# The bias table moved between the forget chunks and the memory attention, two small products put into each of seven k-steps of the first chunk, and three additions of the last stage written for POOL

## The chip, the cores and the metric

One core of a Trainium2 chip runs the whole kernel. The number that counts is device time in microseconds (us) for one execution, from launch to end; it is measured several times on the chip, and the median stands for the kernel. One further execution is recorded by the hardware profiler, and every row below is from that one. Engines are named as the profile names them: PE (TensorE), DVE (VectorE), ACT (ScalarE), POOL (GpSimd), SP (SyncE, which only issues transfers here).

## The reference

A transformer block on 512 tokens of width 1024, all in float32. Three branches read the same x: a dilated band attention with a relative-position bias, a gated linear recurrence (HGRN), and an attention to a memory of 256 rows. Their gated sum is normalised, goes through a mixture of 32 experts (two per token), and is normalised again.

```python
proj = x @ w_in[l]
o_a  = dilated attention of pa with bias = rel_bias[bucket[i, j], head]
o_b  = hgrn2(pb): f = lb + (1 - lb) * sigmoid(f_raw); logf = log(f); bc = cumsum(logf)
o_c  = softmax(pc . k / sqrt(128)) . v        # k, v = mem @ w_kv, 4 heads
merged = gate0 * (o_a @ w_a) + gate1 * (o_b @ w_b) + gate2 * (o_c @ w_c)
x = layer_norm(DN_ALPHA * x + merged @ w_out)
x = layer_norm(DN_ALPHA * x + moe(x))         # two experts per token
```

## The kernel before

The layout is transposed: features lie on the 128 partitions, tokens on the free axis. Each product in full precision is made of three products of halves: a value `v` is split into `h` (rounded to fp32r on ACT, helper `split`, L83) and `l = v - h` (DVE, L84), and `product` adds h·h, h·l and l·h. So a weight chunk of 128 output columns (`proj`, L131) is a 512 KB load on SP's queue, one cast on ACT, one subtraction on DVE and 24 matmuls of 128x512 on PE. The tile pool `wp` gives the chunks rotating buffers (three for each half, four for the raw weights).

The program's order around the change:

- **Start.** Ten products of a zero tile (L151), then x is loaded in eight pieces `xr`; after each one its two halves are made and the three matmuls of that k-step of the first forget chunk go into `acc0` (L166).
- **Forget stage.** Seven more forget chunks. Each ends in a sigmoid (`forget`, L244) and later a logarithm (`log_sums`, L249) on ACT. The two functions need different tables, and ACT loads one before each (16 ACT_TABLE_LOAD in the stage). The memory's halves `mmh`, `mml` are made in between.
- **Memory attention.** For each of four heads: products q (24 of 128x512), k and v (24 of 128x256 each), then for four pieces of 128 rows scores `sc`, maximum, exponential (ACT L297), transposes and the product with v. Then two gate chunks.
- **Bias table.** In a pool of its own (`a0`, two buffers per tag): five pieces `bk` of a one-hot table come in by two POOL transfers each (L327), are cast on ACT (`bkr`, L329), multiplied with the bias table (PE L331, 12 output rows), copied from PSUM on ACT (`rows`, L333), and written to DRAM (`biasd`, POOL L334); later POOL spreads them from there (`repd`, L339).
- **HGRN.** Pool `b`, whose tiles (`bx`, `batt`, `bq`) lie on the same side of the memory as the tiles of `a0`.
- **Experts**, then the **last stage**: every token block c of 128 rows takes two rows picked back from DRAM, `back[c][0]` and `back[c][1]` (loads L1126). `both(c)` adds the two (L1181). `finish(c)` brings the sum to PSUM by a product with the identity (L1137) and adds the last experts (L1038); `norm_out(c)` is bn_stats (L1143), bn_aggr, a scaled subtraction (L1151) on DVE, and for c < 3 a multiplication on ACT (L1158) and an addition on POOL (L1159). In this stage the order on DVE and PE is the one written (`manual_schedule`); elsewhere the scheduler of the tile framework sets it. Every engine works its own list in order.

Of the kernel before, what the change touches and what calls it, by code (L numbers as in the profile page):

```python
# [10 lines left out]
F32 = mybir.dt.float32  # L11
# [9 lines left out]
NEG = -1.0e30  # L21
# [15 lines left out]
def build(tc, ins, out, dbg=None):  # L37
# [5 lines left out]
    def T(pool, shape, dt=F32, tag=None, **kw):  # L43
        cnt[0] += 1
        tag = tag or f"u{cnt[0]}"
        return pool.tile(list(shape), dt, name=f"{tag}_{cnt[0]}", tag=tag, **kw)
# [108 lines left out]
    with tc.tile_pool(name="xs", bufs=2, side="right") as xsp:  # L155
        for k in range(8):
            r = T(xsp, [128, 512], tag="xr", bufs=8)
            nc.sync.dma_start(r, ins["xT"][:, k, :])
            if k % 4 == 0:
                ws = slice(k * 128, (k + 4) * 128)  # L160
                nc.sync.dma_start(raw0[:, ws], ins["w_in"][36 + 8][:, ws])
                split(w0[0][:, ws], w0[1][:, ws], raw0[:, ws])
            split(xh[:, k, :], xl[:, k, :], r)
            ks = slice(k * 128, (k + 1) * 128)
            for n, (wt, m) in enumerate(((w0[0], xh), (w0[0], xl), (w0[1], xh))):
                TE.matmul(acc0, wt[:, ks], m[:, k, :], start=k == 0 and n == 0, stop=k == 7 and n == 2)  # L166

    lvlf = T(fp, [128, 6, 32], tag="lvl")
    G.dma_start(lvlf, ins["lvl"])
# [98 lines left out]
        log_sums(hd)  # L268


    och = T(op_, [128, 4, 512], F32R, tag="oh4")
    ocl = T(op_, [128, 4, 512], F32R, tag="ol4")
    with cpool:
# [32 lines left out]
    dump("oc", och.bitcast(F32))  # L306
    sgc = [gate(2, cb) for cb in range(2)]

    with tc.tile_pool(name="a0", bufs=2, side="right") as tp:
        tab = T(tp, [97, 12], tag="tab")
        V.memset(tab, 0.0)
        for r0 in (0, 64):
            V.memset(tab[r0:r0 + 33, :], NEG)
            G.dma_start(tab[r0:r0 + 32, :], ins["rel_bias"])
        tabr, tabh = (T(tp, [97, 12], F32R, tag=t) for t in ("tabr", "tabh"))
        S.copy(tabr[0:64, :], tab[0:64, :])
        S.copy(tabh, tab)
        V.tensor_tensor(tabr[64:97, :], tab[64:97, :], tabh[64:97, :].bitcast(F32), op=OP.subtract)  # L320
        for j in range(5):
            w = min(512, 2304 - j * 512)
            js = slice(j * 512, j * 512 + w)
            bk = T(tp, [97, 512], tag="bk")
            V.memset(bk[32:64, :w], 0.0)
            for r0 in (0, 64):
                G.dma_start(bk[r0:r0 + 33, :w], ins["bucket"][:, js])  # L327
            bkr = T(tp, [97, 512], F32R, tag="bkr")
            S.copy(bkr[:, :w], bk[:, :w])  # L329
            pt = bank("sc")  # L330
            TE.matmul(pt[:12, :w], tabr, bkr[:, :w], start=True, stop=True)  # L331
            rows = T(tp, [12, 512], tag="rows")
            S.copy(rows[:, :w], pt[:12, :w])  # L333
            G.dma_start(bias_d[:, js], rows[:, :w])  # L334

    def bias_copies(h):
        for lo, n, g, rows in ((0, 7, 0, 32), (7, 1, 1, 128), (8, 1, 2, 128)):
# [834 lines left out]
    with tc.manual_schedule(engines={mybir.EngineType.DVE, mybir.EngineType.PE}):  # L1172
        accs = [None] * 4

        def begin(c, n):
            if c < 3:
                add_to(accs[c][n], n, x1[:, c, :], True)
            add_up(accs[c][n], c, n, group[:1], c == 3, False)

        def both(c):  # L1180
            V.tensor_tensor(back[c][0], back[c][0], back[c][1], op=OP.add)  # L1181

        def finish(c):
            for n in range(2):
                add_to(accs[c][n], n, back[c][0] if c < 3 else x1[:, c, :], False)
            for n in range(2):
                add_up(accs[c][n], c, n, group[1:], False, True)

        def first(j):
            if j == 2:  # L1190
                accs[0] = [bank("sc"), bank("sc")]
                for n in range(2):
                    begin(0, n)
            else:
                accs[2], accs[1] = [bank("pj"), None], [bank("tr"), None]
                begin(2, 0)
                begin(1, 0)

        ohs = onehot(15)
        yp = T(mp, [128, 2, 1024], F32R, tag="yp")  # L1200
        group.append((ohs, yp))
        gu = gate_up(15, xs, first)
        sg = hidden(gu)
        hT = hidden_T(sg)
        both(0)
        accs[2][1] = bank("pj")
        begin(2, 1)
        dn = [down(15, n, hT) for n in range(2)]
        weighted(yp, dn[0], 15, 0)
        both(1)  # L1210
        weighted(yp, dn[1], 15, 1)
        accs[1][1] = bank("tr")
        begin(1, 1)
        finish(0)
        norm_out(accs[0], 0, False)
        both(2)
        finish(1)
        norm_out(accs[1], 1, False)
        both(3)
        V.tensor_tensor(x1[:, 3, :], x1[:, 3, :], back[3][0], op=OP.add)  # L1220
        finish(2)
        norm_out(accs[2], 2, False)
        accs[3] = [bank("o"), bank("o")]
        for n in range(2):
            begin(3, n)
        finish(3)
        norm_out(accs[3], 3, True)
# [98 lines left out]
```

## Time and profile before

| | us |
|---|---|
| median of three runs | 1138.49 |
| lowest, highest | 1136.7, 1140.42 |
| the profiled execution, its time | 1141.1 |
| its span, first to last instruction | 1138.7 |
| PE busy in it | 1087.6 (96%) |
| DVE, ACT, POOL busy | 492.2, 446.4, 82.6 |

The span is what the rows of the trace add up to; 2.4 us of the execution's time lie outside it. An engine's busy share alone decides nothing: it has to be read stage by stage, with what the engines wait for.

### The profile page before, as it was taken

What the parts mean: (1) busy time and instruction counts of PE and PEld (TensorE: products, weight loads), DVE (VectorE), ACT (ScalarE), POOL (GpSimd) and SP (SyncE); (2) the same over time, 40 slices, a digit from 0 to 9 for tenths busy, and PEclk for the clock granted to TensorE, in tenths of its full rate; (3) what the DMA queues carried; (4) which work ended last, traced back from release to release, by engine and by line L of the source; (5) the groups of instructions that cost most, each with busy time, mean ns of one, the idle gap of its engine ahead of it and who ended that gap; (6) DMA issues with size and microseconds to landing.
All of it is one profiled execution on the core that took longest, in us unless ns stands there. A gap on an engine that the chain in (4) does not pass through costs nothing.

```text
span 1138.7 us, 17136 instructions
## 1 busy us (share of the span) xinstructions
PE 1087.6 (96%) x6859; PEld 782.2 (69%) x6859; DVE 492.2 (43%) x985; ACT 446.4 (39%) x756; POOL 82.6 (7%) x107
## 2 busy tenths in 40 slices
PE   9999989999999999999999999999999999888884
PEld 6788778778888887887887887888776333332332
DVE  5554467777777323223223223336467111111126
ACT  7965556666666433233233233224114111111112
POOL 1000330000000000000000001000051211110003
PEclk9999999999999999999999999999999999999998
DMA  8742442222222432332331323633956999999992
GB/s 281 235 128 78 119 135 66 83 66 75 83 59 67 117 100 64 103 93 64 103 94 54 96 93 112 216 93 112 382 218 225 378 406 408 400 398 406 408 372 79
DMA packets 70482, 201.22 MB, mean 177 GB/s; under 512 B 16924, under 2 KB 19064, under 8 KB 70400
## 3 DMA queue, kind: packets, MB, share of 16 engines
q1 hardware_dynamic: 63216, 183.92, 46.1%
q0 software_dynamic: 7184, 16.17, 4.1%
q8 instruction: 55, 0.90, 0.3%
q14 instruction: 27, 0.22, 0.1%
HBM read 191.54 MB, written 17.81 MB: 184 GB/s over the span
## 4 chain that ended last, share of the span: by engine, by line
PE 80%; DMA 9%; ACT 6%; DVE 3%; issue 1%; POOL 0%; DVEq 0%; SPq 0%; ACTq 0%; POOLq 0%
PE pj L131 50%; PE pj L838 7%; DMA raw<-in_wexp_dram 7%; PE o L1054 4%; PE tr L222 3%; PE pj L765 2%; PE o L765 2%; ACT wh L83 1%; PE o L570 1%; PE sc L542 1%; PE sc L412 1%; ACT L244 1%; PE sc L548 1%; PE o L304 1%; ACT L249 1%
## 5 line engine op out<-in xcount | busy, mean ns | idle before, releaser
L84 DVE TENSOR_TENSOR wl<-raw,wh 128x1024 fp32r<-128x1024 f32 (+1 forms) x129 | 148.0, 1149 | 253.2 <-PE pj L131 188.3
L83 ACT CAST wh<-raw 128x1024 fp32r<-128x1024 f32 (+1 forms) x137 | 132.6, 969 | 234.5 <-PE pj L131 223.9
L131 PE MATMUL pj<-xh,wh 128*128 128x512 f32 x760 | 203.2, 401 | 3.7 <-ACT bw L352 3.5
L131 PE MATMUL pj<-xl,wh 128*128 128x512 f32 x760 | 196.6, 396 | 0.0
L131 PE MATMUL pj<-xh,wl 128*128 128x512 f32 x760 | 189.9, 392 | 0.0
L131 PEld LDWEIGHTS pj<-xh,wl 128*128 128x128 f32 x760 | 142.7, 188 | 31.1
L131 PEld LDWEIGHTS pj<-xh,wh 128*128 128x128 f32 x760 | 139.9, 189 | 33.4 <-ACT bw L352 3.9
L131 PEld LDWEIGHTS pj<-xl,wh 128*128 128x128 f32 x760 | 142.1, 189 | 29.6
L838 PE MATMUL pj<-raw,xs 128*64 128x512 f32 x432 | 118.5, 599 | 6.4 <-DMA raw<-in_wexp_dram 5.3
L838 PEld LDWEIGHTS pj<-raw,xs 128*64 128x64 f32 x432 | 35.1, 136 | 67.8 <-issue 46.0
L1054 PE MATMUL o<-raw,ehT 128*64 128x512 f32 x204 | 54.2, 617 | 1.2 <-ACT ehT L1064 0.5
L198 ACT ACTIVATE esg<-pj 128x256 f32<-128x256 f32 x16 | 6.2, 384 | 124.5 <-PE pj L838 124.5
L199 DVE SCALAR_TENSOR_TENSOR esg<-esg,pj 128x256 f32<-128x256 f32 x16 | 6.7, 420 | 107.3 <-ACT esg L198 107.3
L609 POOL DMA_DIRECT2D x<-in_xc_dram x4 | 2.1, 538 | 549.1 <-ACT oh L83 549.1
L1114 DVE TENSOR_SCALAR yp<-o,wsl 128x512 f32<-128x512 f32 x14 | 10.5, 750 | 65.5 <-PE o L1054 65.4
L1054 PEld LDWEIGHTS o<-raw,ehT 128*64 128x64 f32 x204 | 16.9, 140 | 28.2 <-issue 22.6
L131 PE MATMUL pj<-oh,wh 128*128 128x512 f32 x128 | 33.8, 393 | 1.4 <-issue 1.4
L131 PE MATMUL pj<-ol,wh 128*128 128x512 f32 x128 | 33.7, 393 | 0.0
L131 PE MATMUL pj<-oh,wl 128*128 128x512 f32 x128 | 33.3, 392 | 0.0
L214 DVE SCALAR_TENSOR_TENSOR sg<-sg,pj 128x512 f32<-128x512 f32 x16 | 11.0, 687 | 42.0 <-PE pj L131 42.0
L131 PEld LDWEIGHTS pj<-oh,wh 128*128 128x128 f32 x128 | 24.0, 188 | 6.5 <-issue 1.4
L131 PEld LDWEIGHTS pj<-oh,wl 128*128 128x128 f32 x128 | 24.0, 188 | 5.2
(399 smaller groups left out, 1460.8 us busy)
## 6 DMA issues: line engine op xcount, KB each, us to landing
raw<-in_wexp_dram SPq DMA_DIRECT2D x159, 512.0 KB, 10.8
raw<-in_w_in_dram SPq DMA_DIRECT2D x95, 512.0 KB, 3.6
wh<-in_wexp_dram SPq DMA_DIRECT2D x18, 512.0 KB, 11.0
wl<-in_wexp_dram SPq DMA_DIRECT2D x15, 512.0 KB, 12.2
yd<-merged SPq DMA_DIRECT2D x8, 512.0 KB, 7.0
raw<-in_w_kv_dram SPq DMA_DIRECT2D x8, 512.0 KB, 3.6
raw<-in_w_bb_dram SPq DMA_DIRECT2D x8, 512.0 KB, 3.6
raw<-in_w_out_dram SPq DMA_DIRECT2D x8, 512.0 KB, 3.7
```

The costliest lines, as they stand in the source:

```text
L83: S.copy(h, src)
L84: (eng or V).tensor_tensor(l, src, h.bitcast(F32), op=OP.subtract)
L131: TE.matmul(acc, wt[:, k * 128:(k + 1) * 128], m[:, k, :], start=n == 0, stop=n == 3 * kt - 1)
L222: TE.transpose(pt[:, j * 128:(j + 1) * 128], src[:, j * 128:(j + 1) * 128], ident)
L244: S.activation(nat(f), cls(acc), AF.Sigmoid)
L249: S.activation(f, f, AF.Ln, scale=oml[:, hd:hd + 1], bias=lb[:, hd:hd + 1])
L304: TE.matmul(o[:, cs], v[:, js], pT[:, js], start=j == 0, stop=j == 1)
L412: TE.matmul(sa4[g * 32:(g + 1) * 32, n, j], X[:, 2 + n, gs], X[:, 2 + n, gs], start=True, stop=True)
L542: TE.matmul(s1[g * 32:(g + 1) * 32, i * 256:(i + 1) * 256], qs[0][:, c * 128 + g * 32:c * 128 + (g + 1) * 32], ks[0][:, lows[g] * 128:lows ...
L765: TE.matmul(acc, m[:, k, cs], w[:, j * 512:(j + 1) * 512], start=k == 0 and n == 0, stop=k == 7 and n == 2)
L838: TE.matmul(acc[rows_, :], xs[:, j * 2 + k, rows_], raws[2 * p + q, j][:, k * 512:(k + 1) * 512], start=j == 0 and k == 0, stop=j == 3 and ...
L1054: TE.matmul(acc[rows_, :], hT[:, k * 128 + q * 64:k * 128 + (q + 1) * 64], raws[2 * p + q, 4 + k][:, n * 512:(n + 1) * 512], start=k == 0, ...
```

## The change

Three edits. In the start, after the three matmuls of each of the first seven k-steps, two 128x128 products of `xl` with itself go into the bank `tr`, whose contents nothing reads. The code of the bias table moves, unaltered in its arithmetic, from behind the memory attention to in front of it; its pool is gone: the small tables lie in the constant pool, `bk` and `rows` in three rotating buffers of the gate pool (tag `sg`), and `bkr` in `obl`. In the last stage `both(2)`, `both(3)` and the addition to `x1[:, 3, :]` are written ahead of `hidden` and for POOL.

```diff
             for n, (wt, m) in enumerate(((w0[0], xh), (w0[0], xl), (w0[1], xh))):
                 TE.matmul(acc0, wt[:, ks], m[:, k, :], start=k == 0 and n == 0, stop=k == 7 and n == 2)
+            if k < 7:
+                x0 = xl[:, k, 0:128].bitcast(F32)
+                for j in range(2):
+                    TE.matmul(pt, x0, x0, start=True, stop=True)
...
     for hd in range(NF):
         log_sums(hd)
+    tab = T(cp, [97, 12], tag="tab")
...
+    for j in range(5):
+        w = min(512, 2304 - j * 512)
+        js = slice(j * 512, j * 512 + w)
+        bk = T(gp, [128, 512], tag="sg")[:97]
+        V.memset(bk[32:64, :w], 0.0)
+        for r0 in (0, 64):
+            G.dma_start(bk[r0:r0 + 33, :w], ins["bucket"][:, js])
+        bkr = obl[:97, j, :]
+        S.copy(bkr[:, :w], bk[:, :w])
+        pt = bank("sc")
+        TE.matmul(pt[:12, :w], tabr, bkr[:, :w], start=True, stop=True)
+        rows = T(gp, [128, 512], tag="sg")[:12]
+        S.copy(rows[:, :w], pt[:12, :w])
+        G.dma_start(bias_d[:, js], rows[:, :w])
...
-    with tc.tile_pool(name="a0", bufs=2, side="right") as tp:
-        tab = T(tp, [97, 12], tag="tab")
...
-            G.dma_start(bias_d[:, js], rows[:, :w])
...
         def both(c):
-            V.tensor_tensor(back[c][0], back[c][0], back[c][1], op=OP.add)
+            (V if c < 2 else G).tensor_tensor(back[c][0], back[c][0], back[c][1], op=OP.add)
...
         gu = gate_up(15, xs, first)
+        both(2)
+        both(3)
+        G.tensor_tensor(x1[:, 3, :], x1[:, 3, :], back[3][0], op=OP.add)
         sg = hidden(gu)
...
         norm_out(accs[0], 0, False)
-        both(2)
         finish(1)
         norm_out(accs[1], 1, False)
-        both(3)
-        V.tensor_tensor(x1[:, 3, :], x1[:, 3, :], back[3][0], op=OP.add)
```

The order of instructions that results is known for both kernels; three places follow. In the rows, numbers behind names tell tiles apart, and x8 means eight alike in a row.

**Place 1, the end of the forget stage.** PE before, head 0 of the memory attention: k (mmh, mml with wh_547, wl_548), then v (wh_580, wl_581), then its scores.

```order
L131 MATMUL pj_544<-mmh_210,wh_547 128x256 x8
L131 MATMUL pj_544<-mml_211,wh_547 128x256 x8
L131 MATMUL pj_544<-mmh_210,wl_548 128x256 x8
L131 MATMUL pj_577<-mmh_210,wh_580 128x256 x8
L131 MATMUL pj_577<-mml_211,wh_580 128x256 x8
L131 MATMUL pj_577<-mmh_210,wl_581 128x256 x8
L291 MATMUL sc_615<-ck_543,cq_510 128x256
L291 MATMUL sc_632<-ck_543,cq_510 128x256
```

PE now: the same k, and inside its last eight products the bias piece 1 (L294); then v, and head 1's q (wh_763) where head 0's scores stood.

```order
L131 MATMUL pj_619<-mmh_224,wh_622 128x256 x8
L131 MATMUL pj_619<-mml_225,wh_622 128x256 x8
L131 MATMUL pj_619<-mmh_224,wl_623 128x256 x3
L294 MATMUL sc_548<-ol_13_100,tabr_528 12x512
L131 MATMUL pj_619<-mmh_224,wl_623 128x256 x5
L131 MATMUL pj_652<-mmh_224,wh_655 128x256 x8
L131 MATMUL pj_652<-mml_225,wh_655 128x256 x8
L131 MATMUL pj_652<-mmh_224,wl_656 128x256 x8
L131 MATMUL pj_767<-xh_81,wh_763 128x512 x3
```

The bias product of piece 1 stands behind 19 of k's 24 products, and the last five and all of v stand behind it. ACT before, in the same place: weight casts (L83), the last sigmoid (L244), the last logarithm (L249), then cq, the copy of q out of PSUM (L276 in the code), whose next rows are a weight cast and the copy of k.

```order
L83 CAST wh_580<-raw_578 128x1024
L244 ACT_TABLE_LOAD
L244 ACTIVATE merged_86<-pj_465 128x4x128
L249 ACT_TABLE_LOAD
L249 ACTIVATE merged_86<-merged_86,lb_200,oml_201 128x512
L83 CAST wh_688<-raw_686 128x1024
L276 COPY cq_510<-pj_517 128x512
L83 CAST wh_722<-raw_720 128x1024
```

ACT now, with the copy of the bias rows 0 (L296) and the cast of the bias piece 1 (L292, `ol_13` from `sg_543`):

```order
L248 ACTIVATE merged_86<-pj_479 128x4x128
L296 COPY sg_540<-sc_538 12x512
L83 CAST wh_655<-raw_653 128x1024
L253 ACT_TABLE_LOAD
L253 ACTIVATE merged_86<-merged_86,lb_214,oml_215 128x512
L305 COPY cq_585<-pj_592 128x512
L83 CAST wh_763<-raw_761 128x1024
L292 CAST ol_13_100<-sg_543 97x512
```

The cast of v's weights moved from ahead of the sigmoid to behind it, the rows' copy came in after the sigmoid, and the cast of piece 1 stands behind q1's weight cast. On POOL (no rows shown) the second half of the load of each `bk` from piece 1 on stands behind a write of `rows` to `biasd`: that of piece 1 behind the write of the rows 0, that of piece 2 behind the rows 1, that of piece 3 behind the rows 2.

**Place 2, heads 0 and 1.** PE before, from head 0's scores: products of head 1's q (wh_688) lie between.

```order
L291 MATMUL sc_615<-ck_543,cq_510 128x256
L291 MATMUL sc_632<-ck_543,cq_510 128x256
L222 MATMUL tr_610<-ident_61,cvt_576 128x128 x2
L131 MATMUL pj_692<-xh_81,wh_688 128x512 x8
L291 MATMUL sc_649<-ck_543,cq_510 128x256
L222 MATMUL tr_626<-ident_61,cp_620 128x128 x2
L291 MATMUL sc_666<-ck_543,cq_510 128x256
L222 MATMUL tr_643<-ident_61,cp_637 128x128
L304 MATMUL o_614<-cpt_625,cv_609 128x128 x2
L222 MATMUL tr_643<-ident_61,cp_637 128x128
L131 MATMUL pj_692<-xl_82,wh_688 128x512 x4
L304 MATMUL o_614<-cpt_642,cv_609 128x128 x2
```

PE now, from the last bias product: v1's products end, the scores of head 0 (sc from ck_618) and then those of head 1 (ck_793) follow with few products of head 2's q (pj_942) between.

```order
L294 MATMUL sc_578<-ol_13_100,tabr_528 12x256
L320 MATMUL sc_690<-ck_618,cq_585 128x256
L131 MATMUL pj_827<-mmh_224,wl_831 128x256 x7
L320 MATMUL sc_707<-ck_618,cq_585 128x256
L131 MATMUL pj_942<-xh_81,wh_938 128x512
L320 MATMUL sc_724<-ck_618,cq_585 128x256
L131 MATMUL pj_942<-xh_81,wh_938 128x512 x5
L226 MATMUL tr_701<-ident_61,cp_695 128x128 x2
L131 MATMUL pj_942<-xh_81,wh_938 128x512
L320 MATMUL sc_741<-ck_618,cq_585 128x256
L333 MATMUL o_689<-cpt_700,cv_684 128x128 x2
L226 MATMUL tr_718<-ident_61,cp_712 128x128 x2
```

Head 0's scores moved behind head 1's q, k and v; heads 2 and 3 stand as before.

**Place 3, the last stage.** DVE before, from the second `both` on; x is `x1`, raw are the picks:

```order
L1152 RECIPROCAL lnsd_9066<-lnsd_9066 128x1
L1181 TENSOR_TENSOR raw_8912<-raw_8912,raw_8913 128x1024
L1143 BN_STATS lnst_9085<-tr_9011 128x6
L1143 BN_STATS lnst_9085<-tr_9051 128x6
L1145 BN_AGGR lnmv_9088<-lnst_9085 128x2
L1151 SCALAR_TENSOR_TENSOR raw_9092<-tr_9011,lnmv_9088,raw_8922 128x512
L1151 SCALAR_TENSOR_TENSOR raw_9092<-tr_9051,lnmv_9088,raw_8922 128x512
L1152 RECIPROCAL lnsd_9090<-lnsd_9090 128x1
L1181 TENSOR_TENSOR raw_8914<-raw_8914,raw_8915 128x1024
L1220 TENSOR_TENSOR x_1015_6480<-x_1015_6480,raw_8914 128x1024
L1143 BN_STATS lnst_9110<-pj_9010 128x6
L1143 BN_STATS lnst_9110<-pj_9032 128x6
```

DVE now, in the same place:

```order
L1155 RECIPROCAL lnsd_9074<-lnsd_9074 128x1
L1146 BN_STATS lnst_9092<-tr_9016 128x6
L1146 BN_STATS lnst_9092<-tr_9059 128x6
L1148 BN_AGGR lnmv_9095<-lnst_9092 128x2
L1154 SCALAR_TENSOR_TENSOR raw_9099<-tr_9016,lnmv_9095,raw_8927 128x512
L1154 SCALAR_TENSOR_TENSOR raw_9099<-tr_9059,lnmv_9095,raw_8927 128x512
L1155 RECIPROCAL lnsd_9097<-lnsd_9097 128x1
L1146 BN_STATS lnst_9115<-pj_9015 128x6
L1146 BN_STATS lnst_9115<-pj_9040 128x6
```

POOL now, where before the first row was the addition of `norm_out(0)`:

```order
L1119 DMA yd_69<-yp_8757,yidx_6489 1024x1024
L1119 DMA yd_69<-yp_8836,yidx_6489 1024x1024
L1119 DMA yd_69<-yp_8897,yidx_6489 1024x1024
L1184 TENSOR_TENSOR raw_8917<-raw_8917,raw_8918 128x1024
L1184 TENSOR_TENSOR raw_8919<-raw_8919,raw_8920 128x1024
L1208 TENSOR_TENSOR x_1010_6485<-x_1010_6485,raw_8919 128x1024
L1162 TENSOR_TENSOR raw_9076<-raw_9076,raw_8931 128x512 x2
L1162 TENSOR_TENSOR raw_9099<-raw_9099,raw_8931 128x512 x2
```

Three instructions left DVE's list, and the three stand on POOL ahead of its first addition for `norm_out`.

## Rows read from the trace of the kernel before

**Rows 1.** The cores: span and mean granted TensorE clock.

```profile
core 0: 1138.7 us, clock 0.993
```

**Rows 2.** The chain that ended last: its shares by engine.

```profile
PE 80%; DMA 9%; ACT 6%; DVE 3%; issue 1%; POOL 0%; DVEq 0%; SPq 0%; ACTq 0%; POOLq 0%
```

**Rows 3.** Windows: stretch, length, busy by engine, PEclk, DMA share, GB/s.

```profile
15.00:64.00 49.00, 47.80 (x218) 38.64 (x217) 29.83 (x44) 47.93 (x54) 0.00 (x0) 1.00 0.69 228
...
80.00:125.00 45.00, 45.00 (x292) 38.76 (x291) 22.51 (x58) 23.59 (x57) 0.00 (x0) 1.00 0.34 106
...
151.00:153.00 2.00, 2.00 (x6) 1.60 (x5) 2.00 (x7) 0.00 (x0) 1.04 (x3) 0.50 0.85 254
...
1123.30:1126.30 3.00, 2.93 (x8) 1.43 (x8) 2.93 (x7) 0.34 (x2) 1.08 (x1) 1.00 0.40 145
```

**Rows 4.** Timeline: start, duration, what [idle before it, releaser]; start of HGRN.

```profile
145.32 0.43 DVE L376 TENSOR_TENSOR bx<-merged 128x256 f32<-128x256 f32 x1 [4.19 <-ACT wh L83]
...
148.08 1.07 ACT L352 COPY bw<-pj 128x512 f32<-128x512 f32 x1
...
149.21 3.29 PE L131 MATMUL pj<-xh,wh 128*128 128x512 f32 x8 [3.51 <-ACT bw L352]
152.29 2.44 PE L131 MATMUL pj<-xl,wh 128*128 128x512 f32 x8
154.57 2.00 PE L131 MATMUL pj<-xh,wl 128*128 128x512 f32 x8
```

**Rows 5.** Timeline of ACT, the first sigmoid.

```profile
16.63 1.08 ACT L244 ACTIVATE merged<-pj 128x512 f32<-128x512 f32 x1
```

**Rows 6.** Timeline, end of the forget stage (PE and ACT).

```profile
60.39 1.18 PE L131 MATMUL pj<-mmh,wh 128*128 128x256 f32 x8 [0.40 <-ACT merged L244]
...
62.31 1.07 PE L131 MATMUL pj<-mmh,wl 128*128 128x256 f32 x8
...
63.94 1.19 PE L131 MATMUL pj<-mmh,wh 128*128 128x256 f32 x8 [0.56 <-ACT cq L276]
...
64.73 0.37 ACT L280 COPY ck<-pj 128x256 f32<-128x256 f32 x1
```

**Rows 7.** Timeline of ACT in the bias stage, and the landing times of the bias loads.

```profile
129.32 0.61 ACT L329 CAST bkr<-bk 97x512 fp32r<-97x512 f32 x1
...
139.19 0.58 ACT L333 COPY rows<-sc 12x512 f32<-12x512 f32 x1
...
DMA to landing us min/median/max: 2.1/2.6/3.3
```

**Rows 8.** Timeline of ACT, the scores of head 0.

```profile
68.45 1.28 ACT L297 ACT_TABLE_LOAD   x1
69.74 0.47 ACT L297 ACTIVATE cp<-sc,cm 128x256 f32<-128x256 f32 x1
...
72.38 0.47 ACT L297 ACTIVATE cp<-sc,cm 128x256 f32<-128x256 f32 x1 [0.58 <-DVE cm L294]
```

**Rows 9.** Timeline of the last stage (DVE, PE, POOL, SP), and its transfers: size, us to landing.

```profile
1100.15 1.59 SPq L1126 DMA_DIRECT2D raw<-yd  x2
...
1102.71 0.33 SPq L1129 DMA_DIRECT2D raw<-in_ln_dram  x1
...
1119.84 1.21 DVE L1181 TENSOR_TENSOR raw<-raw,raw 128x1024 f32<-128x1024 f32 x1
...
1120.76 3.62 POOL L1159 TENSOR_TENSOR raw<-raw,raw 128x512 f32<-128x512 f32 x2 [1.44 <-ACT raw L1158]
1121.08 2.17 DVE L1220 TENSOR_TENSOR x<-x,raw 128x1024 f32<-128x1024 f32 x1
...
1123.31 1.98 PE L1137 MATMUL o<-x,ident 128*128 128x512 f32 x4 [2.47 <-DVE x L1220]
...
1127.05 2.49 POOL L1159 TENSOR_TENSOR raw<-raw,raw 128x512 f32<-128x512 f32 x2 [2.67 <-ACT raw L1158]
...
raw<-yd SPq DMA_DIRECT2D x8, 512.0 KB, 10.1
```

More of the change, by code (lines that the diff above doesn't have):

```diff
@@ L268, in build @@
         log_sums(hd)
+    tab = T(cp, [97, 12], tag="tab")
+    V.memset(tab, 0.0)
+    for r0 in (0, 64):
+        V.memset(tab[r0:r0 + 33, :], NEG)
+        G.dma_start(tab[r0:r0 + 32, :], ins["rel_bias"])
+    tabr, tabh = (T(cp, [97, 12], F32R, tag=t) for t in ("tabr", "tabh"))
+    S.copy(tabr[0:64, :], tab[0:64, :])
+    S.copy(tabh, tab)
+    V.tensor_tensor(tabr[64:97, :], tab[64:97, :], tabh[64:97, :].bitcast(F32), op=OP.subtract)
+    for j in range(5):
[3 more added lines that the diff above has]
+        V.memset(bk[32:64, :w], 0.0)
+        for r0 in (0, 64):
+            G.dma_start(bk[r0:r0 + 33, :w], ins["bucket"][:, js])
[6 more added lines that the diff above has]
+        G.dma_start(bias_d[:, js], rows[:, :w])
     och = T(op_, [128, 4, 512], F32R, tag="oh4")
@@ L307, in build @@
     sgc = [gate(2, cb) for cb in range(2)]
-    with tc.tile_pool(name="a0", bufs=2, side="right") as tp:
-        tab = T(tp, [97, 12], tag="tab")
[L313 to L333, printed above, removed]
-            G.dma_start(bias_d[:, js], rows[:, :w])
     def bias_copies(h):
```

## The prediction, made before the changed kernel ran

> **What bounds the kernel now.** I read the cores first: one core, granted clock 0.993 over a span of 1138.7 us [rows 1]. Then the chain that ended last: PE holds 80% of it, DMA 9%, ACT 6%, DVE 3%, POOL 0% [rows 2]. So what counts is where PE stops, and the few places where another engine ends last. The windows show three such places that the change touches [rows 3]. From 15 to 64 us ACT is busy 47.93 of 49 us and PE 47.80: both are full, and an instruction added to ACT there can cost its length. From 80 to 125 us, in the memory attention, PE is busy 45.00 of 45. The third place is the pair of short holes: the start of HGRN, where the timeline shows a wait of 3.51 us before PE's product at 149.21 [rows 4], and the last stage, where nearly everything hangs on DVE [rows 9].
>
> **The hole at the start of HGRN.** DVE's first `bx` starts only at 145.32 after 4.19 us idle, ACT's copy `bw` runs 148.08 to 149.15, and PE starts again at 149.21 [rows 4]. The tiles of pool `b` take the place of those of `a0`, so `bx` waits until the last write of `rows` has left the memory; ACT's exponentials wait for `bx`, the copies stand behind them in ACT's list, and PE needs a bank that the copy frees. The second cost is the clock: from 151 to 153 us the granted clock is 0.50, the lower of the two levels, right after that idle time [rows 3]. The eight products at 149.21 take until 152.29, those at 152.29 until 154.57, where the next eight take 2.00 in the rows and 1.83 from start to start (an estimate from 2.00 less the overlap of about 0.17 that the rows show) [rows 4]. That is 3.08 - 1.83 + 2.28 - 1.83 = 1.70 us. The place costs 3.51 + 1.70 = 5.2 us. With the bias table made early, nothing but the end of the attention holds `bx`, and three casted weight chunks lie ready there. I take the whole 5.2 off; the bounds are 5.2 and, if the lateness only moves on to the next ACT wait, 3.0. The five bias products themselves stay on PE and only move.
>
> **What the new place costs.** *Piece 1.* Its product stands behind 19 of head 0's 24 k products and needs its cast on ACT. Sixteen of these took from 60.39 to 62.31 and three more about 0.4, so PE arrives at 62.8 [rows 6]. ACT reached the copy `ck` at 64.73, with the same three casts of weights and the same last sigmoid, logarithm and `cq` copy before it that now stand before piece 1; new in its list are the tables' casts and piece 0 (about 1.0 us, from 0.61 for a piece), against which one weight cast of 1.05 moved from ahead of the sigmoid to behind it, so the sigmoid ends where it did, the copy of the rows 0 (0.58, some 0.48 from start to start) and piece 1 (0.61) [rows 6, 7]. It is cast at 64.73 + 0.48 + 0.61 = 65.8. The transfer is not later: its second half leaves after the rows 0, about 61.5, and lands 2.1 to 3.3 us on [rows 7]. So PE waits 65.8 - 62.8 = 3.0 us. The wait of 0.56 for `cq` before v goes with it [rows 6]: +2.5. Behind the product stand k's last five and all of v, so nothing fills the hole. Bounds: 1.0, if ACT gets ahead, and 4.5, where the 1.0 us of new casts ends late as well and the clock falls (below).
>
> *The table of the exponential.* Before, its load of 1.28 at 68.45 lay under head 1's q [rows 8]. Now it stands behind the copy of the rows 4, whose product is one row ahead of head 0's first score; PE has eight products and two scores before it needs the bank of the first score back. Copy (0.4, an estimate from 0.58 for twice the width [rows 7]), load and first exponential take 0.4 + 1.28 + 0.47 = 2.15 on ACT, and the work ahead of the wait on PE about 1.2 (eight of 256 columns or so by the 1.07 of eight [rows 6]): +1.0 (0 to 1.5).
>
> *Heads 0 and 1 together.* Two exponentials leave ACT every 72.38 - 69.74 = 2.64 us [rows 8]: eight pieces take 10.6 us, about what PE has to do in that stretch. Before, a head's pieces lay among the other's projections and PE never stopped [rows 3]. I take +0.8, between 0 and 3.
>
> *Pieces 2 to 4* have 24 products or more between them, over 3 us each, more than the landing of 3.3 plus the cast of 0.61 less ACT's lead; taken at 0, bound 3 each if it is late as piece 1 is.
>
> **The start.** The two small products after each k-step fill holes in PE's list; what follows the chunk is its sigmoid at 16.63, behind ACT's own list and not behind PE (no wait stands in its row) [rows 5], and the stage after it has ACT full from end to end [rows 3]. The clock is full there already. I take 0 (0 to +0.5; a gain is excluded by the clock).
>
> **The last stage.** DVE loses two additions like that of 1.21 at 1119.84 and the one of 2.17 at 1121.08: 4.59 us, less some 0.2 of overlap, 4.4 [rows 9]. The addition at 1121.08 is that long because POOL works at the same time: its pair at 1120.76 takes 3.62 where 2.49 is normal. So three additions of 1024 elements cost POOL 2.49 to 3.62 each. Picks land 10.1 us after issue: the sixth (issued by 1097.6, an estimate from eight at 1.3 apart ending with the two at 1100.15) at 1107.7, the eighth at 1101.4 + 10.1 = 1111.5. POOL ends at 1110.2, 1114.0 and 1116.5, or 1111.3, 1115.1 and 1118.7. PE wants the first at 1115.7 and the third, which before held it 2.47 us until 1123.31 [rows 9], about 1119.2. It fits, by 0.5 at the worst. I take -4.1, since PE follows closely behind DVE once it no longer waits. Bounds -4.4 and 0.
>
> [...]
>
> From the rows alone, too, `both(1)` may take 2.17 beside POOL's first addition, 1 us more. It lies in front of the second half of the last weighted result, which PE needs about 1 us after it is made now; I price it at 0, and at +1 in the range.
>
> **The sum.** -5.2 + 2.5 + 1.0 + 0.8 - 4.1 = -5.0 us, against this execution's 1141.1: 1136.1. It lies 2.6 us above the median of 1138.49, so for the median I say 1133.5. About 0.3%, 3.4 us, is what a measurement here can tell from no change: the line between faster and same is at 1135.1.
>
> **The rivals.**
> - *All of it hides* (0.17): ACT keeps a lead and piece 1 waits for nothing. For it: the stage before ends as it did. Against: the cast's place behind q1's weight. -5.2 - 4.1 = -9.3: 1129.2.
> - *The clock falls in the new hole* (0.13). 3.0 us lies between 2.47, after which the clock stayed at 1.00 from 1123.3 on, and 3.51, after which it was 0.50 [rows 3, 4, 9]. Then +1.7 (the price above) and a longer wait of 1: -5.0 + 2.7 = -2.3: 1136.2, no change.
> - *POOL's additions come late* (0.12). If the first of them is held until the last of the stage's loads lands (issued 1102.7 [rows 9], so 1112.8), three at 3.62 end at 1123.7, when DVE's addition ended before: the tail gains nothing. -5.0 + 4.1 = -0.9: 1137.6, no change.
> - *Every piece is late as the first* (0.10), the slower side. Each second half is issued only behind the copy of the rows before, so transfer, ACT's list and PE form one loop. Four waits of 3.0 give 12, three more than the sum holds: -5.0 + 9.0 = +4.0: 1142.5. It decides where the loop takes over 6 us a piece, PE's work between pieces 2 and 3; issue, landing, cast, product and copy are 0.5 + 3.3 + 0.6 + 0.4 + 0.6 = 5.4, so it needs ACT's list to be behind as well.
> - The start's products changing something by the clock: it is at 1.00 in the stages after, so I give it no chance of its own.
>
> **How the numbers follow.** Forecast 0.45 (its own range -3 to -7: 1131.5 to 1135.5), the rivals as given, 0.03 left over. Faster: 0.45 less a little plus 0.17 makes 0.60; same 0.28; slower 0.12. The range from 1128.0 (just beyond the case that hides all) to 1139.5 (beyond the cases of no change) leaves out the slower rival and some of the edges.
>
> **What the changed profile would show.** No wait of PE near 149 and a granted clock of 1.00 from 145 to 160, with `bx` on DVE right after head 3. A PE wait of about 3 us for ACT's cast of piece 1 (line 292) inside head 0's k; a second of about 1 for the first exponential. The three additions on POOL (lines 1184, 1208) ended by 1119 on the old clock, and no PE wait for the last. What would make me wrong: ACT's forget stage longer than before, PE waits all through heads 0 and 1, or DVE's own instructions stretched next to POOL.

## The result, and the profile after

| | before | changed |
|---|---|---|
| median, us | 1138.04 (6 runs) | 1146.35 (6 runs, 1145.38 to 1147.29) |
| ratio, 95% interval | | 1.0072 [1.0059, 1.0085] |
| profiled execution: time, span | 1141.1, 1138.7 | 1146.42, 1144.7 |

The change made the kernel slower by 0.72%, 8.3 us. The prediction said 1133.5, in the range 1128.0 to 1139.5.

The cores of the changed kernel; the granted clock is higher than in [rows 1]:

```profile
core 0: 1144.7 us, clock 0.997
```

Its chain that ended last, shares by engine, against [rows 2]: "issue", time in which the engine waited for nothing that the profile shows, went from 1% to 7%.

```profile
PE 77%; DMA 12%; issue 7%; DVE 2%; ACT 1%; POOL 0%; DVEq 0%; ACTq 0%; POOLq 0%; SPq 0%
```

Its windows, with the columns of [rows 3]. The third is the stretch in which the old hole at the start of HGRN lay: PE is busy all through it, at the full clock. In the second, which was full before, PE now loses 1.74 us.

```profile
15.00:64.00 49.00, 48.31 (x212) 38.82 (x213) 30.17 (x50) 47.93 (x56) 1.04 (x2) 1.00 0.69 235
80.00:125.00 45.00, 43.26 (x286) 37.37 (x285) 22.45 (x60) 25.49 (x61) 7.82 (x15) 1.00 0.45 130
125.00:160.00 35.00, 35.00 (x166) 28.25 (x166) 23.22 (x54) 18.60 (x33) 2.79 (x4) 1.00 0.28 88
```

The timeline of ACT in the start, then of PE up to the end of head 0's scores: the waits for x in front of the casts, the second chunk's start, k's first product (at 60.39 before [rows 6]), and every wait of PE that is new there.

```profile
12.38 0.62 ACT L83 CAST xh<-xr 128x512 fp32r<-128x512 f32 x1 [1.02 <-DMA xr<-in_xT_dram]
14.79 1.14 ACT L83 CAST xh<-xr 128x512 fp32r<-128x512 f32 x2 [1.80 <-DMA xr<-in_xT_dram]
...
17.91 2.02 PE L131 MATMUL pj<-xh,wh 128*128 128x512 f32 x8
...
62.98 1.11 PE L131 MATMUL pj<-mmh,wh 128*128 128x256 f32 x8
...
67.56 0.41 PE L294 MATMUL sc<-ol,tabr 97*12 97x512 f32 x1 [2.16 <-ACT ol L292]
...
74.74 0.41 PE L294 MATMUL sc<-ol,tabr 97*12 97x512 f32 x1 [1.18 <-ACT ol L292]
...
84.88 0.29 PE L294 MATMUL sc<-ol,tabr 97*12 97x256 f32 x1 [0.88 <-ACT ol L292]
87.97 0.70 PE L320 MATMUL sc<-ck,cq 128*128 128x256 f32 x2 [0.87 <-ACT cp L326]
```

The last stage, against [rows 9] (DVE's two additions left, POOL's three, PE's product with x, and DVE's last scaling, which before started at 1129.20):

```profile
1114.13 1.23 DVE L1184 TENSOR_TENSOR raw<-raw,raw 128x1024 f32<-128x1024 f32 x1
...
1119.25 1.22 DVE L1184 TENSOR_TENSOR raw<-raw,raw 128x1024 f32<-128x1024 f32 x1
...
1119.39 3.30 POOL L1184 TENSOR_TENSOR raw<-raw,raw 128x1024 f32<-128x1024 f32 x1 [33.56 <-DMA raw<-yd]
...
1123.08 2.36 POOL L1184 TENSOR_TENSOR raw<-raw,raw 128x1024 f32<-128x1024 f32 x1 [0.39 <-PE sc L1041]
...
1125.51 2.37 POOL L1208 TENSOR_TENSOR x<-x,raw 128x1024 f32<-128x1024 f32 x1
...
1129.70 1.88 PE L1140 MATMUL o<-x,ident 128*128 128x512 f32 x4
...
1135.16 1.53 DVE L1159 SCALAR_TENSOR_TENSOR raw<-raw,lnsd,raw 128x512 f32<-128x512 f32 x2
```

No step that the prediction priced lost 8 us. Two things stand where it had no term. First the projections: the costliest groups of the page of before (line, tiles, count, busy us, mean ns of one):

```profile
L131 PE MATMUL pj<-xh,wh 128*128 128x512 f32 x760 | 203.2, 401 | 3.7 <-ACT bw L352 3.5
L131 PE MATMUL pj<-xl,wh 128*128 128x512 f32 x760 | 196.6, 396 | 0.0
L131 PE MATMUL pj<-xh,wl 128*128 128x512 f32 x760 | 189.9, 392 | 0.0
```

and of the changed kernel:

```profile
L131 PE MATMUL pj<-xh,wh 128*128 128x512 f32 x760 | 204.9, 402 | 0.0
L131 PE MATMUL pj<-xl,wh 128*128 128x512 f32 x760 | 197.7, 397 | 0.0
L131 PE MATMUL pj<-xh,wl 128*128 128x512 f32 x760 | 192.5, 395 | 0.0
```

The same 2280 products take 5.4 us longer, although the stretch at half clock is gone from the first group. From start to start, eight of them take 1.83 us before and 1.86 after, all through the kernel; one pair of each, before and after:

```profile
20.87 2.00 PE L131 MATMUL pj<-xh,wh 128*128 128x512 f32 x8
22.70 1.99 PE L131 MATMUL pj<-xl,wh 128*128 128x512 f32 x8
...
141.35 2.03 PE L131 MATMUL pj<-xh,wh 128*128 128x512 f32 x8
143.21 2.02 PE L131 MATMUL pj<-xl,wh 128*128 128x512 f32 x8
```

Second, in HGRN, waits of PE, most of them before short products, that nothing in the profile releases (after):

```profile
228.50 0.41 PE L419 MATMUL sc<-bx 128*32 128x32 f32 x14 [1.57 <-issue]
...
289.14 0.51 PE L422 MATMUL sc<-bx 128*64 128x64 f32 x6 [1.64 <-issue]
...
354.33 0.26 PE L419 MATMUL sc<-bx 128*32 128x32 f32 x5 [1.28 <-issue]
...
371.17 0.26 PE L415 MATMUL sc<-bx 128*32 128x32 f32 x5 [0.62 <-issue]
```

Before there were two:

```profile
227.22 0.85 PE L131 MATMUL pj<-oh,wh 128*128 128x512 f32 x3 [1.36 <-issue]
...
252.97 0.33 PE L412 MATMUL sc<-bx 128*32 128x32 f32 x16 [1.16 <-issue]
```

So the span's 6.0 us divide like this (stages cut at the first and the last transposition of `bw` and at the first pick of the last stage): up to HGRN +1.7 (158.09 for 156.40), HGRN +5.1 (224.95 for 219.89), from there to the last stage +4.7, last stage -5.4.

### The profile page after: what moved, and what is told of

Same layout as the page of the kernel before. It is cut to its first block, busy times and chain, and to the rows that moved or that the text cites. A ratio compares the mean times of both kernels' runs of the same rounds, so it can differ in the third digit from the quotient of the medians.

```text
span 1144.7 us, 17184 instructions
## 1 busy us (share of the span) xinstructions
PE 1094.1 (96%) x6887; PEld 785.7 (69%) x6887; DVE 487.8 (43%) x982; ACT 446.0 (39%) x756; POOL 89.4 (8%) x110
## 4 chain that ended last, share of the span: by engine, by line
PE 77%; DMA 12%; issue 7%; DVE 2%; ACT 1%; POOL 0%; DVEq 0%; ACTq 0%; POOLq 0%; SPq 0%
PE pj L131 50%; DMA raw<-in_wexp_dram 11%; PE pj L841 5%; PE tr L226 3%; PE o L1057 3%; PE pj L768 2%; PE o L768 2%; PE o L573 1%; PE sc L545 1%; PE sc L415 1%; PE sc L551 1%; PE o L333 1%; PE sc L723 1%; PE o L581 1%; PE o L454 1%
## 5 line engine op out<-in xcount | busy, mean ns | idle before, releaser
L83 ACT CAST wh<-raw 128x1024 fp32r<-128x1024 f32 (+1 forms) x137 | 132.4, 968 | 242.0 <-PE pj L131 227.2
L131 PE MATMUL pj<-xh,wl 128*128 128x512 f32 x760 | 192.5, 395 | 0.0
L131 PEld LDWEIGHTS pj<-ol,wh 128*128 128x128 f32 x128 | 23.9, 188 | 5.5
```

Of the source, the lines that this page charges most:

```text
L83: S.copy(h, src)
L131: TE.matmul(acc, wt[:, k * 128:(k + 1) * 128], m[:, k, :], start=n == 0, stop=n == 3 * kt - 1)
```

## The experiments

A is the start's products, B the move of the bias table, C the last stage. "Place" means the address of pool `wp` in SBUF, the on-chip memory, given as bytes per partition behind where it lay before; "pace" is the time of one product of 512 columns. The theory was that the tables' 192 bytes (three tiles, taken at 64 each) in the constant pool push pool `wp`, which holds `raw`, `wh` and `wl`, and the pools behind it, to addresses where products run slower; the rivals were that the slower pace or the loss comes from the moved instructions themselves.

**1. The place alone.** The kernel before, and one tile that nothing uses; the instructions of all engines are those of before.

```diff
+    pad = T(cp, [128, 48], tag="pad")
```

> The kernel before, with 192 bytes per partition more in the constant pool (an unused tile): no instruction is added and every engine's list is as before; only the tiles of the pool behind it, the weight halves and the raw weights, lie 192 bytes further on, as in the changed kernel. Theory P (the place of the weight tiles sets the pace of the products of 512 columns): a run of eight takes 1.86 to 1.87 us from start to start in place of 1.83, and with about 2660 such products at 3.8 to 5 ns more each the kernel takes 9 to 11 us more, 1147 to 1149. Rival Q (the pace comes from something the changed kernel executes, such as the start's products or another order): 1.83 us and 1138.

1146.12 us, 1.0073 [1.0046, 1.0100]. Its groups:

```profile
L131 PE MATMUL pj<-xh,wh 128*128 128x512 f32 x760 | 205.7, 404 | 3.7 <-ACT bw L353 3.5 <-ACT wh L83 0.2
L131 PE MATMUL pj<-xl,wh 128*128 128x512 f32 x760 | 199.6, 399 | 0.0
L131 PE MATMUL pj<-xh,wl 128*128 128x512 f32 x760 | 192.6, 395 | 0.0
```

That is 8.2 us more than before in these rows, with the wait for `bw` in both; the half clock behind that wait lasts 6.9 us here and 3.4 before, which by an estimate (half of the difference, as the 3.4 before cost 1.70 by [rows 4]) is 1.7 of the 8.2. From start to start eight products take 1.87. An unused tile of 192 bytes per partition costs as much as the whole change.

**2. The change with the place put right.** 64 bytes more, so that `wp` stands 256 behind its old address.

```diff
+    pad = T(cp, [128, 16], tag="pad")
```

> The changed kernel with 64 bytes more in the constant pool, so that the weight tiles lie 256 bytes further on than before instead of 192. Theory P, if what counts is the place within 256 bytes: 1.83 us for eight products and about 10 us less than the changed kernel, 1136. Theory P with another period: 1.86 and 1146, or something between. Rival Q: 1.86 and 1146.

1139.05, 1.0008 [0.9992, 1.0024], not the 1136 of the theory, but the pace is that of before (1.83 us for eight). The place is worth 1.0072 - 1.0008 = 0.0064, 7.3 us, in the changed kernel too.

**3. A alone.**

```diff
+            if k < 7:
+                x0 = xl[:, k, 0:128].bitcast(F32)
+                for j in range(2):
+                    TE.matmul(pt, x0, x0, start=True, stop=True)
```

> The kernel before with the first edit alone: two products of x with itself after each of seven k-steps. Theory: no effect, 1138 within 0.3%, second chunk starting within 0.5 us of 15.26, since PE's holes take them. Rival: they are what delays the second chunk by 2.65 us in the changed kernel, 1140 to 1141. Rival Q in its form that the start's products slow the pace of all later ones: 1148.

1140.25, 1.0021 [1.0005, 1.0038]: not nothing, and not at the start, where the second chunk begins at 15.72 against 15.26. HGRN takes 222.59 against 219.89 and has four waits without a releaser (1.68, 1.74, 0.83, 0.42).

**4. C alone.**

```diff
-            V.tensor_tensor(back[c][0], back[c][0], back[c][1], op=OP.add)
+            (V if c < 2 else G).tensor_tensor(back[c][0], back[c][0], back[c][1], op=OP.add)
...
+        both(2)
+        both(3)
+        G.tensor_tensor(x1[:, 3, :], x1[:, 3, :], back[3][0], op=OP.add)
...
-        both(2)
...
-        both(3)
-        V.tensor_tensor(x1[:, 3, :], x1[:, 3, :], back[3][0], op=OP.add)
```

> The kernel before with the third edit alone: the two additions of picks and the one to x1 on POOL. Theory: the last stage gains what the changed trace shows, 4 to 4.7 us, 1133.5 to 1134. Rival (POOL late without the later start of the changed kernel, or transfers in the way): 1 us or nothing, 1137 to 1138.

1132.87, 0.9962 [0.9948, 0.9977]: -4.3 us by the ratio, as the term of -4.1 said.

**5. The change without A, with the place put right** (the tile of 2, and the lines of 3 taken out).

> The changed kernel with the weight tiles at +256 bytes and without the start's products. Theory: PE pauses of 1.3 to 1.7 us for which the profile names no releaser come at fixed places of PE's own list (matmul 1261 and 1687 of it in four traces); the 14 products more moved them from long products to HGRN's small ones. Without them only the pause before matmul 1261 is seen, as in the kernel before, and the second chunk starts about 0.5 us earlier: 2.5 to 3 us less than the run at +256 bytes with them, 1136. Rival (the pauses hang on the bias table or on POOL's transfers): the pauses stay, 1138.5 to 1139.

1134.06, 0.9965 [0.9954, 0.9976]. The second chunk starts later than in 2, not earlier (17.69 against 17.03). Only one wait without a releaser is left, of 1.42 at 254.29. By the ratios A costs 4.9 us beside B and C, twice its 2.4 alone.

**6. B alone, with the place put right.**

> The kernel before with the second edit alone, weight tiles at +256 bytes. Theory: the table's move is worth nothing or costs, since the start loses 1.5 to 2 us to its loads, piece 1 and the scores wait 3 to 4 us and the hole of 3.5 us and its slow clock are gone: 1138 to 1141. Rival (the move gains as forecast, -0.9 us or more, and the loss lies in the pauses alone): 1136.5 to 1138.

1140.32, 1.0015 [1.0005, 1.0025]. The hole at the start of HGRN is gone, and four waits in the attention (2.62, 0.89, 1.33, 1.05) and a second chunk that starts at 18.16 against 15.26, with 3.4 us at half clock around it, give more than it back.

**7. As 5, with the early loads on SP's queue behind x.** The small table's and piece 0's loads no longer share the start with x on POOL's queue.

```diff
-        G.dma_start(tab[r0:r0 + 32, :], ins["rel_bias"])
+        nc.sync.dma_start(tab[r0:r0 + 32, :], ins["rel_bias"])
...
-            G.dma_start(bk[r0:r0 + 33, :w], ins["bucket"][:, js])
+            (nc.sync if j == 0 else G).dma_start(bk[r0:r0 + 33, :w], ins["bucket"][:, js])
```

> As the run without the start's products, with the loads of the small table and of piece 0 on SP's queue, where they stand behind x and the first weight chunks, instead of on POOL's queue beside x. Theory: they are what slowed x's loads; the second chunk starts at 15.0 to 15.5 instead of about 16.5 to 17, 1 to 2 us less than the run without the start's products. Rival (x's loads vary by themselves): no difference beyond 0.5 us.

1134.36, 0.9972 [0.9959, 0.9984], no faster than 5. The second chunk starts at 16.83 instead of 17.69, and the waits for the pieces take it back (2.49, 1.22, 1.24, 1.03). The start alone settles little: in this trace PE runs at half clock from 14.0 to 17.4, which the trace of 5 does not have there, and the kernel of 5 starts that chunk at 17.13 in its other trace (12).

**8 and 9. The place at 64 and at 128 bytes**, in the kernel of 4 (an unused tile of 16 or of 32 numbers).

> The last stage's edit alone, with 64 bytes more in the constant pool. Theory P in the form that the place within 128 bytes decides: 1.86 us for eight products as at +192, 1142 to 1143. In the form that only some places within 256 are bad (+192 is one): 1.83 and 1133, or a third value that shows how the pace follows the place.

> The last stage's edit alone, weight tiles at +128 bytes. So far eight products of 512 columns took 1.83 us at +0 and +256, 1.81 at +64, 1.86 at +192. Theory P with a period of 128 (as +64 differs from +192, it would have to fail): 1.83 and 1133. With a period of 256: a value of its own, and the time follows it at 2660 products: 1126 to 1148 as it is 1.80 to 1.87.

At 64 bytes 1128.53, 0.9915 [0.9897, 0.9933]; at 128 bytes 1141.88, 1.0027 [1.0013, 1.0040]. The groups at 64:

```profile
L131 PE MATMUL pj<-xh,wh 128*128 128x512 f32 x760 | 202.6, 400 | 4.3 <-ACT bw L353 3.5 <-ACT wh L83 0.8
L131 PE MATMUL pj<-xl,wh 128*128 128x512 f32 x760 | 195.9, 395 | 0.0
L131 PE MATMUL pj<-xh,wl 128*128 128x512 f32 x760 | 188.4, 390 | 0.0
```

At 128 they are those of 1 (205.9, 199.1, 192.9). Eight products take 1.81 and 1.87 from start to start. So an address can also help: the place of before was not the fastest one.

**10. The bias table behind head 1.** C, the tile of 64 bytes, and the code of B behind head 1 of the attention in place of the end of the forget stage, its tables and four buffers for `bk` in the attention's own pool.

```diff
+            bk = T(tp, [128, 512], tag="bk", bufs=4)[:97]
...
+            if h == 1:
+                bias_table()
```

> The last stage's edit, weight tiles at +64, and the bias table behind head 1 of the memory attention, with four buffers of its own for its pieces in that stage's pool, so that no load waits for a write. The scheduler puts the casts into the forget stage and the products among head 1's transposes. Theory (the move's cost is the loads beside x, the loop of load, cast and product, and the late table of the exponential, none of which is here; left are 3 us of casts on a full ACT): the hole of 3.5 us and its slow clock go, 5.2 less and 3 more than the run at +64 with the last stage alone, 1126 to 1127. Rival (whatever takes the table forward costs as much as it gains): 1128.5 or more.

1123.66, 0.9879 [0.9851, 0.9907], the fastest kernel of the study: 1.2% under the kernel before. No bias product waits, PE is busy 35.00 of 35 us from 125 to 160, and the first transposition of `bw` starts at 152.78, in 8 at 158.51, where the hole is followed by 6.9 us at half clock.

**11. Fourteen products of zeros** with 32 columns ahead of the k-steps, in the kernel of 8; nothing reads them. Like the fourteen of A they stand in the trace as 28 matmuls and 28 weight loads (6887 matmuls for 6859).

```diff
+    for j in range(14):
+        TE.matmul(pt[:, :32], idle, idle[:, :32], start=True, stop=True)
```

> The run at +64 with the last stage alone, and 14 products of 32 columns of the zero tile behind the ten at the start, before any data is there: the same number of matmuls more in PE's list as the first edit adds, at no place where they could hold anything. Theory (pauses lie at fixed counts of PE's list): the pauses show in HGRN's small products again, 4 of them in place of 2, and the kernel takes 2.5 to 5 us more, 1131 to 1133.5. Rival (the first edit's loss lay in the k-steps or in chance): 1128.5.

1130.73, 0.9930 [0.9902, 0.9958]: 2.2 us over 8, but the two intervals overlap. The trace has four waits without a releaser (2.06, 1.99, 0.98, 0.54) where 8 has two (1.08, 1.51).

**12 to 15. A count or a start?** Four kernels side by side on one chip: that of 5; with A (that of 2); with fourteen idle products as in 11; with twenty-eight.

> The changed kernel without the fourteen start products, with 64 bytes more in the constant pool; the base for the three runs beside it. Both theories: as when it ran before, ratio to the kernel before 0.9965, about 1134; in the HGRN stage one or two waits of PE that no releaser explains, together 1.4 to 2.6 us.

> The same kernel with the fourteen start products in it (two after each of seven k-steps, products of xl). The theory of the list (fourteen more entries in PE's list shift where its unexplained waits fall): slower than the base beside it by 3 to 5 us, with four unexplained waits in the HGRN stage that sum to about 5.5 us. The theory of the start (the products delay the k-steps or the clock): slower by as much, but the loss is there at the end of the forget stage already, and the HGRN stage is as long as in the base.

> The base with fourteen products of a zero tile with 32 columns, ahead of the k-steps, while PE has nothing else to do; their result is read by nothing. The theory of the list: the same loss as with the start products, 2.5 to 5 us over the base, four unexplained waits in the HGRN stage at the same instructions as there. The theory of the start: as the base, within 1 us.

> The base with twenty-eight such products of zeros. The theory of the list: the waits stand at the same counts of PE's list and so fourteen instructions earlier in the program again than with fourteen; their number and sum differ from both others (between 1 and 7 us in all), and the time follows that sum. A theory in which each added product costs its own time: twice the loss of fourteen. The theory of the start: as the base, within 1 us.

| | median, us | ratio to before, interval | HGRN, us | waits without a releaser, us |
|---|---|---|---|---|
| no start products | 1134.28 (10 runs) | 0.9965 [0.9954, 0.9976] | 219.81 | 1.32, 1.16 |
| A | 1139.74 (12) | 1.0010 [0.9998, 1.0022] | 224.09 | 1.66, 1.79, 1.46, 1.32 |
| 14 idle | 1138.31 (12) | 1.0001 [0.9988, 1.0015] | 222.95 | 1.64, 1.74, 0.79, 0.99 |
| 28 idle | 1140.47 (12) | 1.0012 [1.0000, 1.0023] | 222.99 | 2.32, 1.86 |

The waits with A, and below those with twenty-eight idle products:

```profile
226.67 0.41 PE L420 MATMUL sc<-bx 128*32 128x32 f32 x14 [1.66 <-issue]
...
286.92 0.51 PE L423 MATMUL sc<-bx 128*64 128x64 f32 x6 [1.79 <-issue]
...
351.66 0.26 PE L420 MATMUL sc<-bx 128*32 128x32 f32 x5 [1.46 <-issue]
...
369.13 0.26 PE L416 MATMUL sc<-bx 128*32 128x32 f32 x5 [1.32 <-issue]
```

```profile
204.50 0.68 PE L421 MATMUL sc<-bx 128*64 128x64 f32 x8 [2.32 <-issue]
...
368.57 0.19 PE L414 MATMUL sc<-bx 128*32 128x32 f32 x1 [1.86 <-issue]
```

Fourteen products that do nothing cost 4.1 us by the ratios, against 5.1 for A, with intervals that overlap, and they bring waits before the same kinds of instructions. Twenty-eight cost 5.4, not twice 4.1, and their waits stand elsewhere. For fourteen the start doesn't explain it: with A the first transposition of `bw` comes at 156.89, with fourteen idle products at 157.55, without at 157.23. What counts for these waits here is how many instructions stand ahead in PE's list, not what they do. With twenty-eight the waits are only 1.7 us longer in sum than without any (4.18 for 2.48). The traces show the rest: there the idle products run until 14.4 us, the granted clock is at the half level from 8.6 to 18.8, the second chunk starts at 21.92 against 17.13, and HGRN starts 2.7 us later; and behind the last wait the clock is at half from 370.4 to 373.8, about 1.7 us by an estimate (half of 3.4). So with twenty-eight the theory of the start is in part right.

Around these waits the profile's instruction queue is at work. In the run with A of 13, one line for each of the stretches 224 to 225, 227 to 229 and 283 to 285 us (packets, MB, share):

```profile
q8 instruction: 1, 0.02, 7.1%
...
q8 instruction: 1, 0.02, 3.5%
...
q8 instruction: 1, 0.02, 4.2%
```

A packet starts between 224 and 225, no other until 227, and PE stands from about 225.0 to 226.67 in between; the packet of 283 to 285 is followed by the wait that ends at 286.92. The kernel without A has a packet between 285 and 286 too, and no wait there. The traces show more than that. Number all of PE's records (weight loads, matmuls and the few others) of a trace in order from 0: in the seventeen traces together there are 42 waits of over 0.3 us without a releaser, 0.4 to 2.3 us each, all of them at or right behind products of 32 to 128 columns. Each ends at a record whose number leaves 193 or 194 when divided by 256 (before at 3265 and 3777; in the changed kernel at 3265, 4545, 5825 and 6337), and 1.2 to 1.6 us after a packet of 16 KB on this queue has ended. The 56 records of fourteen products move other instructions to these numbers. So these waits stand whole multiples of 256 records apart, give or take one, and PE goes on about 1.4 us after a packet has ended; why only some packets are followed by a wait (2 of 55 before, 4 of 55 in the changed kernel), all of them among the short products, and what a packet holds, is not shown.

## Why the prediction was wrong

By the ratios, each step with the ones before it in place:

| | ratio | us of 1139 |
|---|---|---|
| C alone (4) | 0.9962 | -4.3 |
| with B, place put right (5, 12) | 0.9965 | +0.3 |
| with A (13) | 1.0010 | +5.1 |
| with the place as it came out | 1.0072 | +7.1 |

Sum: +8.2, of a measured 8.3. Each ratio is uncertain by 1.3 to 1.7 us, so B's +0.3 can't be told from nothing; alone (6) it cost 1.7. The prediction had -4.1, -0.9 (B: -5.2 + 2.5 + 1.0 + 0.8), 0 and nothing.

- **The step that failed is the list of the change's parts**: it held instructions, waits and transfers, and not the place of tiles. The small tables' move into the constant pool stood in the description of the change and got no price; it is the largest term, 7.1 us, and experiment 1 shows it alone. Nothing in the rows of before could have given its size. A row that shows 2664 products of one kind (2280 and three times 128) at one pace could have told how much hangs on that pace: 1% of their 229 ns each is 6.1 us.
- **"The start. I take 0 (0 to +0.5)"** was the second error: 1.5 to 2.4 us alone, 5.1 in company. The argument about what follows the chunk was right, the products cost nothing there. They cost it 200 us later, in HGRN (+4.3 us beside the same kernel without them), through the count of PE's list. Two waits of that kind stood in the trace of before, at 227.22 and 252.97, and I passed over them since the change does not touch HGRN.
- **The hole at the start of HGRN** (-5.2): mechanism right. The wait of 3.51 and the half clock are gone [rows 3, 4]; its size is not shown by itself, since no run takes the hole away without B's other costs.
- **Piece 1** (+2.5): mechanism right. It waits 2.16, the copy's wait of 0.56 is gone: +1.6. ACT ends the cast at 67.51 behind the row copy, v's and q1's weight casts, in the order read from its list.
- **Pieces 2 to 4** (0): two of the three wait, 1.18 and 0.88. In the timeline of ACT their casts wait for the load of `sg` by 1.25 and 2.04, so the transfers behind the row copies are late, which the bound of "late as piece 1" allowed for. The slower side's loop does not close: piece 3 waits for nothing.
- **The exponential's table** (+1.0): 0.87. **Heads 0 and 1 together** (+0.8): no wait behind 87.97 in that stretch. The sum of all new waits less the 0.56 is 4.5, against 4.3; that these agree is luck, since two terms were too large by 1.7 together and pieces 2 to 4, taken at 0, wait 2.1.
- **Not seen**: the start of the second chunk, 17.91 against 15.26. ACT waits for x [first of the rows above], while POOL's queue moves 400 packets in the first 18 us instead of 192, among them the bias loads, which now are issued there. In the runs with the early table it stands at 16.8 to 18.2 (21.9 with twenty-eight idle products), in the others at 14.8 to 16.0. Taking the loads off POOL moved the start by 0.9, little more than it varies, and the time not at all (7). Whether the transfers or ACT's new casts are the cause is not settled.
- **The last stage** (-4.1): right, -4.3 alone. POOL's third addition ends at 1127.88; DVE's first `both` starts at 1114.13 against 1103.49 before, so that is 1117.2 on the old clock, inside the forecast's 1116.5 to 1118.7. PE's product with x has no wait before it, and DVE's last scaling comes 5.4 us nearer to the first pick's load, some of it more than the term: from `both(1)` to that scaling it is 15.91 for 20.37, 4.5 us less, and 15.90 to 16.03 in all thirteen traces with C. `both(1)` took 1.22 beside POOL's 3.30 (2.36 for the same shape alone), so the 1 us that the range held for it did not appear here. It did in others: in six of those thirteen DVE's addition started first, took 1.22 or 1.23, and POOL's took 3.21 to 3.30; in seven POOL's started first and took 2.36, and `both(1)` took 2.62 to 3.27. The one that starts second is stretched, and it cost the tail nothing.
- **The rivals**: in the trace of the changed kernel the clock did not fall in the new hole, though PE waited 2.16 (no stretch at half clock until the last stage, 0.997 over the run). With the same table at the place of 256 it did in five of eight traces: in 2, 5, 12, 13 and 14 PE waited 2.40 to 2.63 for piece 1, and around the end of that wait, from 66 to 70 us on, the clock stood at half for 3.4 us (6.9 in 14); in 6 and 7, after 2.62 and 2.49, it stayed full. So that rival is real, and its price of 1.7 us is part of what B cost in those five. The additions were not late, and the pieces were not all late. None of the rivals holds the 7.1 us of the place or the 5.1 of A.

## What to carry to other kernels

Where a kernel spends most of its time in one kind of product, read from the allocation where its tiles stand before and after, and try a few offsets with an unused tile: here places 64 bytes apart differ by up to 13 us (64 against 128), more than every reordering in this change. Compare two versions only at the same offset, or the place is taken for the edit. And a handful of added instructions, however idle, can cost time far behind them: here fourteen products shifted the places at which a long list of short products stalled (two waits became four, 4.1 us), and twenty-eight held the start and its clock as well (half level from 8.6 to 18.8 us); look for waits that nothing releases, and count them in both traces.

## What the runs showed of the hardware

- **Pace by place.** Mean of one product of 512 columns in the group of `xh` and `wl`, the products being the same in all kernels: at the old place of `wp` 392 ns, 64 bytes on 390, 128 bytes on 395, 192 bytes on 395, 256 bytes on 392. (These means hold the overlap of neighbours; from start to start it is 228.8 ns before and 232.5 at 192.) Times went with it: 0.9962, 0.9915 and 1.0027 at 0, 64 and 128 in one kernel. The first products of the experts (432, into `pj`), with weights straight from `raw` tiles behind `wp`, stayed at 598 or 599 ns in all of these. Which part of the address counts, and which tile carries it, was not tried.
- **Waits without a releaser** of 0.4 to 2.3 us stand among PE's shortest products, at records of PE's list whose number leaves 193 or 194 when divided by 256, 1.2 to 1.6 us after a 16 KB packet of the instruction queue: one or two in the list as it was, four with fourteen products more, two longer ones with twenty-eight.
- **Two additions at once.** Of a DVE and a POOL addition of 128x1024 that ran at the same time, the one that started first kept its length (1.22 or 2.36 us), and the other took 2.62 to 3.30, in all thirteen traces.
